# Sliding windows by DMA: the odd rows of the direct batches in 63 small transfers, each released by SyncE's list

## The chip, the core and the metric

The kernel runs on one core of a Trainium2 chip. No compute engine works on the data: everything is moved by DMA. Three engines issue transfers, each through a queue of its own: SyncE (SP in the profile, queue q1), ScalarE (ACT, queue q10) and GpSimd (POOL, queue q0, whose descriptors are written by software and which the change calls the software ring). All three queues feed the same 16 DMA engines. The metric is device microseconds for one execution of the kernel; three runs of the kernel before took 748.2, 749.22 and 749.88 us, with a median of 749.22.

## The reference

```python
batch, length, dim = (32, 4096, 256)      # float32
window_size, stride = 64, 32
n_windows = (length - window_size) // stride + 1        # 127
for i in range(n_windows):
    start = i * stride
    result[:, i] = x[:, start:start + window_size].copy()
```

A batch of the input is 128 blocks of 32 rows; a block is 32 x 256 floats, 32 KB. Window i is blocks i and i+1, so the output is 32 x 127 windows of 64 KB, 266 MB, and nearly every block is written twice: as the second half ("half 1") of one window and as the first half ("half 0") of the next.

## The kernel before

The 32 batches are done in two ways.

**Staged batches.** Twelve batches (`staged`, line 151) are loaded into SBUF, 4 MiB each, one block to a partition (`load`, line 40), and stored from there twice, once as half 0 and once as half 1 of the windows (`store`, line 49). All of this is issued by ScalarE (`ring_s`) in `Staging.run` (line 121): six tiles are loaded, all six are stored, six more are loaded when their tiles are free, and these are stored. Loads and stores are cut into packets of 16 KB. A store has all 128 partitions, although there are only 127 windows, so that its last row falls on one row of a neighbouring batch. The last two staged batches are stored together by `store_pair` (line 102): four stores that count on the semaphore `spilt`, one more store on `ended`, a wait for `spilt`, and then three more stores on `ended`. A store of the pair is 2 MB.

**Direct batches.** The other twenty batches are copied from HBM to HBM. Of the 127 windows of a batch, 112 go in transfers of 16 windows and one half (`halves`, line 174): 16 pieces of 32 KB, 512 KB in all, 14 transfers for each batch, 280 in all. SyncE (`ring_d`) issues them. Of these, 22 hold a row that a staged store overwrites; they are the list `spoilt` (line 175), and SyncE issues them at its end, each after a wait (`wait_stored`, line 114) for the stores beside it. The last two wait for `spilt`.

**Odd rows.** What is left of a direct batch are 15 windows, numbers 48 to 62, as whole rows of 64 KB. GpSimd (`ring_r`) issues them (`remainder`, line 170): one transfer of 15 rows for each batch, with packets of 32 KB or, for four batches, 16 KB; the last batch's 15 rows are split into one transfer of 11 rows and four of 2 rows and one half. That makes 24 transfers, all issued at the start without any wait.

**Order.** SyncE issues one transfer (line 191), then waits for the semaphore `back` (line 192), which the 15-row transfer of the 17th direct batch sets when it has landed, and then issues the other 257 `halves` and the 22 `spoilt`. An issuing engine is held up when its ring is full, so that SyncE and ScalarE issue at the pace of their transfers; the trace shows a median of 84.0 us from the issue of a SyncE transfer to its landing. At the end SyncE waits for all counts (line 199).

## Time and profile before

| what | value |
|---|---|
| runs, median | 749.22 us (748.2 to 749.88) |
| the profiled execution | 747.93 us, its span 746.1 us |
| moved by the DMA engines | 317.50 MB, 426 GB/s over the span |
| q1, SyncE: packets, MB, share of 16 engines' span | 8960, 146.82, 46.0% |
| q10, ScalarE | 10064, 151.00, 47.6% |
| q0, GpSimd | 1280, 19.66, 6.2% |
| SyncE's wait for `back` | 83.2 us |
| from issue to landing, median | SyncE 84.0 us; GpSimd's 15 rows 44.1 us; ScalarE's loads of 4096 KB 121.2 us |

The page counts MB by the packets: a copy from HBM to HBM counts once, and a staged block counts once when it is loaded and once for each store. Small packets of 4 B are the semaphore updates, which travel in the same queues. Besides the views that the page prints, the trace keeps a record of every packet with its queue, start, size and duration; where a number is said to be from the packet records, it is the mean or the sum over these.

### The profile page before, as it was taken

What the parts mean: (1) busy time and instruction counts of PE and PEld (TensorE: products, weight loads), DVE (VectorE), ACT (ScalarE), POOL (GpSimd) and SP (SyncE); (2) the same over time, 40 slices, a digit from 0 to 9 for tenths busy, and PEclk for the clock granted to TensorE, in tenths of its full rate; (3) what the DMA queues carried; (4) which work ended last, traced back from release to release, by engine and by line L of the source; (5) the groups of instructions that cost most, each with busy time, mean ns of one, the idle gap of its engine ahead of it and who ended that gap; (6) DMA issues with size and microseconds to landing.
All of it is one profiled execution on the core that took longest, in us unless ns stands there. A gap on an engine that the chain in (4) does not pass through costs nothing. (4 is left out here: it accounts for less than half of the span.)

```text
span 746.1 us, 413 instructions
## 1 busy us (share of the span) xinstructions
POOL 13.8 (2%) x28
## 2 busy tenths in 40 slices
POOL 7000000000000000000000000000000000000000
DMA  8999999999999999999999999999999999999997
GB/s 365 425 427 417 430 417 432 430 429 435 436 421 432 428 434 434 428 430 432 434 407 427 431 434 429 436 433 428 429 433 432 430 431 431 430 432 433 431 431 336
DMA packets 20306, 317.50 MB, mean 426 GB/s; under 512 B 5880, under 2 KB 5880, under 8 KB 5880
## 3 DMA queue, kind: packets, MB, share of 16 engines
q10 hardware_dynamic: 10064, 151.00, 47.6%
q1 hardware_dynamic: 8960, 146.82, 46.0%
q0 software_dynamic: 1280, 19.66, 6.2%
q14 instruction: 2, 0.02, 0.0%
HBM read 216.79 MB, written 267.12 MB: 649 GB/s over the span
## 5 line engine op out<-in xcount | busy, mean ns | idle before, releaser
L34 POOL DMA_DIRECT2D out_dram<-in_x_dram x24 | 13.6, 571 | 1.1 <-PEq L231 1.1
L217 POOL MEMSET const-float32-0.0<- 128x1 f32 x1 | 0.1, 98 | 0.2 <-issue 0.2
L217 POOL MEMSET const-bfloat16-1.0<- 128x1 bf16 x1 | 0.1, 101 | 0.0
L217 POOL MEMSET const-float32-1.0<- 128x1 f32 x1 | 0.1, 98 | 0.0
L217 POOL MEMSET const-uint8-127<- 128x1 uint8 x1 | 0.1, 98 | 0.0
## 6 DMA issues: line engine op xcount, KB each, us to landing
out_dram<-in_x_dram SPq DMA_DIRECT2D x280, 512.0 KB, 84.0
out_dram<-xb ACTq DMA_DIRECT2D x28, 2048.0 KB, 106.2
xb<-in_x_dram ACTq DMA_DIRECT2D x11, 4096.0 KB, 121.2
out_dram<-xb ACTq DMA_DIRECT2D x10, 4096.0 KB, 120.8
out_dram<-in_x_dram POOLq DMA_DIRECT2D x19, 960.0 KB, 44.1
xb<-in_x_dram ACTq DMA_DIRECT2D x4, 1024.0 KB, 13.9
out_dram<-in_x_dram POOLq DMA_DIRECT2D x1, 704.0 KB, 84.7
out_dram<-in_x_dram POOLq DMA_DIRECT2D x4, 64.0 KB, 69.2
```

The lines of the kernel that those rows point to most:

```text
L34: return q.dma_start(out=self.oap((b * self.nw + w0) * 2 + h, [[2 * blk, n], row]), in_=self.xap(b * self.nb + w0 + h, [[blk, n], row]), m ...
L217: nc = _bacc.Bacc("TRN2", target_bir_lowering=False, num_devices=1)
```

## The change

The 24 transfers of GpSimd become 63 (`drip`): 59 of whole rows, nearly all of them 5 rows, and four of one half of 3 or 5 rows (the entries named a and b in `plan`, whose second half comes later in the list). A row of 64 KB is one packet. The first is issued at once; every other one waits for a semaphore of its own (`marks`), which one of SyncE's `halves` sets when it has landed. The marks are spread evenly over the 258 `halves`, one to each 4.1 of them, so that the last one stands at number 253. SyncE no longer waits for `back`. Every fourth of its `halves` (64 of 258) is cut into packets of 16 KB in place of 32 KB. The staged part and the `spoilt` list are as before.

```diff
-    back = tc.alloc_semaphore("back")
-    total = {done: 0, rest: 0, back: 0}
+    total = {done: 0, rest: 0}
 
     def count(dma, sem):
         dma.then_inc(sem, 16)
-        total[sem] += 16
-
-    def blocks(part):
+        if sem in total:
+            total[sem] += 16
+
+    def blocks(part, piece=DIRECT, sem=done):
         for b, w, half in part:
-            count(c.windows(ring_d, b, w, 16, half), done)
-
-    def remainder(i, b, w, n, half=None, piece=DIRECT):
-        count(c.windows(ring_r, b, w, n, half, piece), back if i == len(direct) - 4 and n == 15 else rest)
-
-    first, last = 48, B - 1
+            count(c.windows(ring_d, b, w, 16, half, piece), sem)
+
+    first = 48
...
+    plan = [(5, "")] * 26 + [(2, ""), (3, "a")] + [(5, "")] * 5 + [(5, "b")] + [(5, "")] * 6
+    plan += [(3, "a")] + [(5, "")] * 2 + [(5, "b")] + [(5, "")] * 19
+    drip, named, at = [], {}, 0
+    for n, name in plan:
+        if name in named:
+            drip.append((*named[name], n, 1))
+            continue
+        b, w = direct[at // 15], first + at % 15
+        drip.append((b, w, n, 0 if name else None))
+        at += n
+        if name:
+            named[name] = b, w
+    assert at == 15 * len(direct)
+    marks = [tc.alloc_semaphore(f"mark{i}") for i in range(len(drip) - 1)]
+    at = [len(halves) * (i + 1) // len(drip) for i in range(len(marks))]
+
     with tc.tile_critical():
         st.run(ring_s)
 
-        pairs = iter([(first + d, half) for d in (0, 2) for half in (0, 1)])
-        for i, b in enumerate(direct[:-1]):
-            if i in (12, 15, 17, 18):
-                w, half = next(pairs)
-                remainder(i, last, w, 2, half, DIRECT // 2)
-            if i == len(direct) - 2:
-                remainder(i, last, first + 4, 11)
-            remainder(i, b, first, 15, piece=DIRECT // 2 if i in (0, 1, 2, 6) else DIRECT)
+        for i, (b, w, n, half) in enumerate(drip):
+            if i:
+                ring_r.wait_ge(marks[i - 1], 16)
+            count(c.windows(ring_r, b, w, n, half, 2 * DIRECT), rest)
         ring_r.drain()
 
-        blocks(halves[:1])
-        ring_d.wait_ge(back, 16)
-        blocks(halves[1:])
+        for i, h in enumerate(halves):
+            sem = marks[at.index(i)] if i in at else done
+            blocks([h], DIRECT if i % 4 != 2 else DIRECT // 2, sem)
```

## The prediction

> **What bounds the kernel now.** I read the page's slices and queues first, since no compute engine works. The row "DMA" is the busy share of the 16 DMA engines in 40 slices.

> ```profile
> span 746.1 us, 413 instructions
> DMA  8999999999999999999999999999999999999997
> GB/s 365 425 427 417 430 417 432 430 429 435 436 421 432 428 434 434 428 430 432 434 407 427 431 434 429 436 433 428 429 433 432 430 431 431 430 432 433 431 431 336
> q10 hardware_dynamic: 10064, 151.00, 47.6%
> q1 hardware_dynamic: 8960, 146.82, 46.0%
> q0 software_dynamic: 1280, 19.66, 6.2%
> ```

> The engines are full from the second slice to the last but one, and the queues' shares add up to 99.8%. The bound is the engines' own rate. The stretches between the kernel's stages show where it falls short (columns: length, POOL busy, PE clock, DMA share, GB/s):

> ```profile
> 0.00:5.00 5.00, 3.69 (x11) 1.00 0.55 210
> 5.00:98.00 93.00, 10.06 (x18) 1.00 1.01 426
> 98.00:132.00 34.00, 0.00 (x0) 1.00 1.00 418
> 132.00:371.00 239.00, 0.00 (x0) 1.00 1.01 431
> 371.00:383.00 12.00, 0.00 (x0) 1.00 1.03 403
> 383.00:738.00 355.00, 0.00 (x0) 1.00 1.01 431
> 738.00:746.10 8.10, 0.00 (x0) 1.00 0.54 216
> ```

> Undisturbed, it runs at 431 GB/s. At that rate 317.50 MB take 736.7 us. The rest, against 431: start 5 x (431-210)/431 = 2.6 us; 5 to 98 us, ScalarE's loads beside GpSimd's rows, 93 x 5/431 = 1.1; 98 to 132, loads beside SyncE's list, 34 x 13/431 = 1.0; 371 to 383, where ScalarE turns from stores to loads, 12 x 28/431 = 0.8; end 8.1 x 215/431 = 4.0. Together 746.2, the span. No edit of order can win more than these 9.5 us, and about 4 of the start and end are latency ahead of the first packet (2.4 us into the span) and behind the last (1.8 us before its end).

> Then who waits:

> ```profile
> SPq L34 <- DMA out_dram<-in_x_dram: 83.2, 1, 83.2
> SPq L34 <- DMA out_dram<-xb: 43.4, 2, 39.9
> SPq L200 <- DMA out_dram<-xb: 40.5, 1, 40.5
> ```

> SyncE stands 83.2 us at `back`. That costs nothing: in that time the other two queues held the engines at a share of 1.01.

> Last, how the engines share themselves. This is 383 to 738 us, with two queues working:

> ```profile
> DMA packets 9736, 152.98 MB, mean 431 GB/s; under 512 B 2835, under 2 KB 2835, under 8 KB 2835
> q1 hardware_dynamic: 4869, 79.83, 52.4%
> q10 hardware_dynamic: 4866, 73.14, 48.1%
> ```

> The two queues sent the same number of packets (4869 and 4866) though not the same bytes: they take turns, packet by packet, and a 4 B semaphore packet is a turn too. This decides in which order the lists end.

> **The change, part by part.** Durations are from the packet records: clean means of 1.213 us for 32 KB, 0.611 for 16 KB, 0.009 for 4 B; two 16 KB packets cost 0.009 us more than one of 32 KB. One packet starts 3 to 4 ns before the last is over, so a packet costs 6 ns beyond its bytes.

> - The wait for `back` goes. The engines were full during it, so 0. If cover failed it would be up to 83.2 us; what is late next is nothing, since SyncE's ring then holds transfers from the start. Bounds: a gain of 0 to 1.1 us (the shortfall of 5 to 98 us, if the way GpSimd's rows run there makes it).
> - Packets. GpSimd's data packets fall from 728 (1280 less 552 of 4 B) to 308 (292 of 64 KB, 16 of 32 KB): -420. SyncE's rise by 64 x 16 = 1024. GpSimd's 4 B packets are 552/24 = 23 a transfer, so 39 more transfers bring 897. Net +1501, 94 an engine; at 6 to 9 ns that is 0.6 to 0.8 us, all on the path, as the engines are full. I take +0.6.
> - A packet of 64 KB is in no trace. By the slope from 16 to 32 KB it takes 0.611 + 3 x 0.602 = 2.42 us, no gain or loss; from below nothing is to be had beyond the 6 ns counted above. From above, the slowest row of 32 KB packets is the first 16 of the run, 1.498 us, 23% over the clean mean: on 18.25 such packets an engine that would be 18.25 x 2.42 x 0.23 = +10 us. Those were an engine's first packets; the clean row is nearer, so 0.
> - GpSimd's waits. Behind each wait stand only GpSimd's own later transfers and its drain; SyncE's last wait needs them. An issue takes 571 ns (24 of them, 13.6 us) and a mark comes every 4.1 transfers, about 11 us, so the list keeps pace. The last mark, number 253 of 258, comes with 5 `halves` and 22 `spoilt` still to go, 27 x 2.4 us = 65 us before the end. Cost 0; without that cover, the 3.7 us that the fastest transfer took to land.
> - The turns. GpSimd now takes a third place in the round now and then, which slows the other two alike. ScalarE has 576 data packets and 53 of 4 B an engine: 629 turns. SyncE has (194 x 2) + (64 x 3) + (22 x 2) = 624. Before, SyncE and GpSimd together had 560 + 80 = 640 against 629, and SyncE ended last by a little. Now ScalarE should, by some 5 to 8 turns (it also starts later), which is its last store, 8 packets of 0.61 us = 4.9 us alone. The engines are full with one queue as well, so the cost is 0. The cover to name: after `spilt` ScalarE has one 2 MB store in its ring, 9 turns, 5.5 us even alone, while a new issue needs about 3 us (first packet 2.4 us into the span, first ScalarE packet 3.9). If that cover goes, some 1 to 3 us appear as a dent about 40 us before the end.
> - The engines' loads. 300 rows on 16 engines are 18.75 rows each: 37.5 halves, before as after. If consecutive engines are dealt out in a ring, both plans give 38 halves to twelve or thirteen engines and 34 to 37 to the others. So the end's skew stays; bounds -1.2 and +2.4 us, one 32 KB packet less or one 64 KB packet more on the engine that ends last. I take 0.
> - The loads' shortfall (1.1 + 1.0 us up to 132 us, 0.8 at the turn). The slow packets there are mostly ScalarE's loads, just after a new load begins, when all 16 engines start on it at nearly the same time. Groups of five engines with a 64 KB packet pull the engines apart earlier than 15 of 16 did. Bounds: all 2.1 gone, or as much again. I take half a gain, -1.0.

> Sum on the profiled execution: 747.93 + 0.6 - 1.0 = 747.5. It lies 1.29 us under the median of the runs; the median becomes 749.22 - 0.4 = 748.8.

> [...]

> **The rivals.**

> - Shortfall gone (faster). The 2.1 us up to 132 us and the 0.8 at the turn were stalls of engines in step, and the drip takes them out: 749.22 + 0.6 - 2.9 = 746.9; one packet less of skew at the end, 745.7. For it: from 383 us on, loads ran beside SyncE's list at 431. Against: from 98 to 132 they did so at 418.
> - The end slips (slower). The engine that ends last gets one 64 KB packet too many, or gets it late: +2.4, and 749.22 + 0.6 + 2.4 = 752.2. It decides if the last slice (336 GB/s) falls below 320. For it: the last 8.1 us already run at half rate. Against: the last mark is 65 us ahead.
> - GpSimd's rows disturb wherever they run (slower). They read each block twice at nearly the same time. If their mere presence costs the 5 GB/s seen from 5 to 98 us, it is now paid over some 690 us: 690 x 5/431 = 8.0, less the 1.1 paid before, +6.9: 749.22 + 0.6 + 6.9 = 756.7. It decides if the middle slices fall under 430. Against: in proportion to the rows moved, the sum stays 1.1.
> - Same five engines (slower). If 5 rows always land on the same five, each of these carries 120 halves in place of 37.5: +82 x 1.21 = 99 us. Against: 15 rows on a fixed 15 would have left one engine 46 us short of work before, and the share at 383 to 738 us is 1.01 of all 16. The 64 KB packet at the cold price, 760, I put with this.
> - It does nothing: the removed wait was covered. That is my forecast's core.

> **How the numbers follow.** A measurement of this kernel can tell about 0.2%, 1.5 us, from no change (747.7 to 750.7). Chances: forecast 0.42, its own range 747.4 to 750.3; shortfall gone 0.25; the end slips 0.18; rows disturb everywhere 0.10; five engines or slow packets 0.05. Faster: 0.25 and 0.06 of the forecast's lower edge, 0.31. Same: 0.36. Slower: 0.33. A range of 745.7 to 753.0 leaves out the last two cases and a little of the others, 0.19.

> **What would show it.** Right: q0's work spread over all slices, 431 in the middle; q1 and q10 with the same packet counts in any stretch; SP's 83.2 us wait gone without a change of the time; ScalarE's store landing last. Wrong: middle slices under 430, last slices thin, or a span below 744.

## The result and the profile after

The changed kernel took 850.33 us (849.87 to 851.52) against 749.22 for the kernel before: 1.135 times as long, 95% interval 1.1335 to 1.1366, or 101.1 us more. Its profiled execution took 849.87 us, its span 848.1 us. The forecast was 748.8 with a range up to 753.0. The time lies at the rival "same five engines", which had been given 0.05 together with slow packets and would give 749.22 + 0.6 + 99 = 849.

The page after, its slices and queues:

```profile
span 848.1 us, 451 instructions
DMA  9999999999999999999999799999998898843382
GB/s 371 423 430 434 429 424 429 430 435 432 426 428 436 424 424 436 428 424 423 422 402 382 305 349 402 393 378 370 351 417 349 355 392 335 331 195 150 134 358 123
q1 hardware_dynamic: 9984, 146.82, 43.0%
q10 hardware_dynamic: 10064, 151.00, 41.9%
q0 software_dynamic: 2016, 19.67, 5.5%
```

The bytes are the same. For the first half the engines run as before, at some 430 GB/s; from there on they fall off. The stretches say it more sharply (length, POOL busy, PE clock, DMA share, GB/s):

```profile
5.00:98.00 93.00, 3.65 (x7) 1.00 1.01 428
98.00:132.00 34.00, 1.57 (x3) 1.00 1.00 425
132.00:371.00 239.00, 9.92 (x19) 1.00 1.01 429
...
437.00:740.00 303.00, 12.53 (x24) 1.00 0.92 367
740.00:778.00 38.00, 1.57 (x3) 1.00 0.48 186
778.00:798.00 20.00, 0.52 (x1) 1.00 0.31 134
798.00:830.00 32.00, 0.00 (x0) 1.00 0.71 293
830.00:848.10 18.10, 0.00 (x0) 1.00 0.24 102
```

The line to stop at is 778 to 798 us: a share of 0.31 of 16 engines is five engines, working at their full rate (134 GB/s is 5/16 of 430), while eleven stand idle. Against 431 GB/s the five last stretches lose 45, 22, 14, 10 and 14 us, about 105 in all, where the end of the kernel before lost 4.

These are SyncE's waits after, the ones that answer to those shown of before. The 83.2 us at `back` are gone, and that bought nothing:

```profile
SPq L34 <- DMA out_dram<-xb: 66.7, 4, 44.4
SPq L209 <- DMA out_dram<-xb: 36.5, 1, 36.5
```

How many engines lag can be read from the semaphores. Each mark is set by one transfer of SyncE, 16 pieces of 32 KB with 16 updates (4480 packets of 4 B for 280 transfers), and the trace keeps the time of each update. Which engine one came from it does not say; they are read here as one from each engine. These are the 16 updates of some marks of the changed kernel, in order, as us after the first of them:

```
mark at   the 16 updates, us after the first
 15.1     0.0 0.0 0.0 0.1 0.2 0.2 0.2 0.3 0.3 0.5 0.8   2.1  2.2  2.3  2.4  2.4
 24.7     0.0 0.1 0.1 0.1 0.2 0.2 0.2 0.2 0.3 0.4 0.6   4.7  4.8  4.8  4.8  5.3
 34.9     0.0 0.1 0.1 0.2 0.3 0.3 0.4 0.4 0.5 0.6 0.8   6.8  6.9  7.0  7.2  7.7
 44.8     0.0 0.0 0.1 0.2 0.2 0.2 0.3 0.3 0.3 0.4 0.6   9.3  9.3  9.4  9.6 10.0
423.9     0.0 0.1 0.2 0.2 0.3 1.0 1.0 1.3 1.7 2.2 2.7  88.1 91.1 91.3 93.2 93.6
690.7     0.0 0.1 0.2 0.2 0.2 0.2 0.3 0.3 0.3 0.3 0.6  82.2 88.3 89.3 89.7 90.0
```

Eleven engines are together and five fall behind, by one 64 KB packet (2.4 us) more with every transfer of GpSimd. So every transfer gives its five rows to the same five engines. The lag grows to some 90 us and stops there. What stops it can be counted from the packet records: SyncE's packets that are issued and not yet done when an issue ends. In the kernel before this number rises while an issue takes 0.59 us (median from 85 to 110 us); from 130 to 600 us it stands at 1110 to 1121 (median 1112), while an issue takes 2.39 us and a transfer 84 us to land: that is what lies in a ring. In the changed kernel it reaches 1090 at 31 us and is down to 354 to 437 from 437 to 690 us (median 398), not far above five sixteenths of 1112, 348; from 437 to 740 us SyncE issues a transfer only every 3.0 us (101 in 303 us). On this count the five have a full ring, SyncE's issue is held up for all 16, and the eleven run dry. The marked transfers show it: one whose issue ended at 111.4 us had its first update 55.5 us later and its last 95.2 us later; one whose issue ended at 420.1 us had them after 3.7 and 97.2 us. From then on eleven engines have next to no queue, and five have a full one. That is why the first half of the profile looks healthy.

### The profile page after: what moved, and what is told of

It is laid out like the page before. It is cut to its first block, busy times and chain, and to the rows that moved or that the text cites. A ratio compares the mean times of both kernels' runs of the same rounds, so it can differ in the third digit from the quotient of the medians.

```text
span 848.1 us, 451 instructions
## 1 busy us (share of the span) xinstructions
POOL 33.2 (4%) x67
## 3 DMA queue, kind: packets, MB, share of 16 engines
q1 hardware_dynamic: 9984, 146.82, 43.0%
q10 hardware_dynamic: 10064, 151.00, 41.9%
## 4 chain that ended last, share of the span: by engine, by line
another core or an unknown queue 79%; DMA 5%; POOL 4%; issue 3%; SPq 1%; POOLq 0%
DMA out_dram<-in_x_dram 5%; POOL out_dram L34 4%; SPq L34 1%; POOLq L198 0%; SPq L240 0%; SPq L191 0%
## 5 line engine op out<-in xcount | busy, mean ns | idle before, releaser
L34 POOL DMA_DIRECT2D out_dram<-in_x_dram x63 | 33.0, 524 | 748.0 <-DMA out_dram<-in_x_dram 747.0
```

The costliest lines, as they stand in the source:

```text
L34: return q.dma_start(out=self.oap((b * self.nw + w0) * 2 + h, [[2 * blk, n], row]), in_=self.xap(b * self.nb + w0 + h, [[blk, n], row]), m ...
```

## Experiments

What was open is why the deal of rows to engines, which turned in the kernel before, stood still here: the packet, the wait before each transfer, or the number of rows. On the chips of the experiments the kernel before took 746.3 to 746.7 us, not 749.22, so every run is read against the kernel before beside it. The changed kernel itself was not run there. A time without an interval is one execution.

### Packets of 32 KB

```diff
-            count(c.windows(ring_r, b, w, n, half, 2 * DIRECT), rest)
+            count(c.windows(ring_r, b, w, n, half, DIRECT), rest)
```

> The changed kernel with GpSimd's rows cut into packets of 32 KB again; the 63 transfers, their waits and SyncE's list stay. All theories agree that 60 x 64 KB rows fall on the same five engines in the changed kernel (120 halves in place of 37.5, 82 x 1.21 = 99 us). They differ in why the deal stopped turning. Packet theory (a row that is one 64 KB packet is always dealt from the same engine): 749 us here, within 3. Wait theory (a transfer that is issued alone, after a wait, starts the deal anew): 850, unchanged. Row theory (a transfer of 5 rows always takes the same five): 850, unchanged.

751.92 us beside 746.73. The 98 us are gone with the packet, and with them the wait theory and the row theory: waits and five rows are still there. The first three marks show the deal move on by five engines with each transfer: five engines are some 2.4 us behind the others at the first mark, ten at the second, fifteen at the third. But 5.2 us stay. The stretches of this run show five engines once more, only for a short while at the end:

```profile
700.00:740.00 40.00, 0.00 (x0) 1.00 1.00 426
742.00:745.00 3.00, 0.00 (x0) 1.00 0.32 137
```

The marks date it. Up to 317 us the 16 updates lie within 4.5 us; then five engines fall behind, to about 10 us at 512 us, where the eleven others lie within 3. The transfers released at that time are those of one half, entries a and b of `plan`. Their rows are 32 KB, so with packets of 32 KB they still have one packet to a row. If they fall on the same first engines, the fullest carries 4 of these 16 halves in place of 1, which is 3 x 1.21 = 3.6 of the 5.2 us.

### No waits

```diff
-    marks = [tc.alloc_semaphore(f"mark{i}") for i in range(len(drip) - 1)]
-    at = [len(halves) * (i + 1) // len(drip) for i in range(len(marks))]
...
         for i, (b, w, n, half) in enumerate(drip):
-            if i:
-                ring_r.wait_ge(marks[i - 1], 16)
             count(c.windows(ring_r, b, w, n, half, 2 * DIRECT), rest)
...
         for i, h in enumerate(halves):
-            sem = marks[at.index(i)] if i in at else done
-            blocks([h], DIRECT if i % 4 != 2 else DIRECT // 2, sem)
+            blocks([h], DIRECT if i % 4 != 2 else DIRECT // 2, done)
```

> The changed kernel with GpSimd's 63 transfers all issued at the start, no wait and no mark; 64 KB packets and SyncE's cut list stay. Wait theory: the deal turns again, 749 us, within 3. Packet theory and row theory: the same five engines still carry 120 halves, 850 us, within 10.

850.42 us beside 746.73, 103.7 us more; with the waits it was 101.1 more, on another chip. The deal stood still here too, though no transfer waited for another to land. The lag comes earlier, and so does the hole, but the sum of the work on the five is the same:

```profile
98.00:371.00 273.00, 0.00 (x0) 1.00 0.84 347
...
800.00:810.00 10.00, 0.00 (x0) 1.00 0.32 136
```

### 15 rows in packets of 64 KB

```diff
-                remainder(i, last, first + 4, 11)
-            remainder(i, b, first, 15, piece=DIRECT // 2 if i in (0, 1, 2, 6) else DIRECT)
+                remainder(i, last, first + 4, 11, piece=2 * DIRECT)
+            remainder(i, b, first, 15, piece=2 * DIRECT)
```

> The kernel before with its transfers of 15 and 11 rows in packets of 64 KB. Packet theory: the same 15 engines each time, one engine is left without rows and the others carry 40 halves in place of 38: 749.2 + 2 x 1.21 = 751.6 us. Wait theory and row theory: the deal turns as before, 748 to 750.

757.1 us beside 746.73. The direction is that of the packet theory, but the size is 10.4 us where 2.4 were expected. One engine is left without rows: towards the end the share is 15 of 16, 0.94.

```profile
5.00:98.00 93.00, 9.16 (x18) 1.00 1.00 405
...
690.00:720.00 30.00, 0.00 (x0) 1.00 0.94 403
720.00:738.00 18.00, 0.00 (x0) 1.00 0.95 396
738.00:755.00 17.00, 0.00 (x0) 1.00 0.62 266
```

The first line holds part of what the expectation lacked: with 64 KB packets on 15 engines beside ScalarE's loads the first stretch ran at 405 GB/s (426 in the kernel before), 93 x 21/431 = 4.5 us. The last line holds another part, 17 x 165/431 = 6.5 us, where the end of the kernel before lost 4: ScalarE's last packet ended 13 us behind SyncE's, at 753.5 us. The parts are read from single executions and do not add up to the last microsecond.

### 15 rows with waits

```diff
...
+    marks = [tc.alloc_semaphore(f"mark{i}") for i in range(23)]
+    sent = []
...
     def remainder(i, b, w, n, half=None, piece=DIRECT):
-        count(c.windows(ring_r, b, w, n, half, piece), back if i == len(direct) - 4 and n == 15 else rest)
+        if sent:
+            ring_r.wait_ge(marks[len(sent) - 1], 16)
+        sent.append(n)
+        count(c.windows(ring_r, b, w, n, half, piece), rest)
...
-        blocks(halves[:1])
-        ring_d.wait_ge(back, 16)
-        blocks(halves[1:])
+        at = [len(halves) * (i + 1) // 24 for i in range(23)]
+        for i, h in enumerate(halves):
+            blocks([h], marks[at.index(i)] if i in at else done)
```

> The kernel before with its 24 transfers (15 rows, 32 and 16 KB packets) each released by a mark of SyncE's list, 23 waits evenly spread, and SyncE's wait for back gone; SyncE's packets stay at 32 KB. Wait theory: the same 15 engines each time, one left without rows, 751.6 us. Packet theory and row theory: the deal turns, 748 to 750.

754.68 us beside 746.73: no theory had that. The deal did turn: the updates of the 23 marks stay within 7.3 us of each other, and no engine is far in front of the rest. The loss is another one. In this run SyncE's packets are uncut, its list is early, and it stood 119.1 us at the staged stores. That led to the next runs.

### Every odd row in two packets

```diff
-            count(c.windows(ring_r, b, w, n, half, 2 * DIRECT), rest)
+            count(c.windows(ring_r, b, w, n, half, DIRECT if half is None else DIRECT // 2), rest)
```

> The changed kernel with every odd row in two packets: whole rows as 2 x 32 KB, the four transfers of one half as 2 x 16 KB. Form theory (a transfer of GpSimd with one packet to a row is always dealt to the same first engines; with two packets to a row the deal turns): no engine group lags any more, the marks' 16 landings stay within 4 us of each other, and what is left of the change is worth what the forecast's other terms say, +0.6 for packets and up to -2.1 of the loads' shortfall: between 2 us faster and 1 us slower than the kernel before on this chip. If the drip costs something in itself, as in the first run with 32 KB packets (+5.2), it stays 3 to 5 us slower.

746.25 us beside 746.43: ratio 0.9999, interval 0.999 to 1.0007. With this one expression the 101 us are gone, and the rest of the change, taken together, is worth nothing. From the run with packets of 32 KB this one differs in the four transfers of one half alone, and the 5.2 us are gone too. The 16 updates of each of the 62 marks lie within 5.1 us. The stretches and, from 383 to 680 us, the queues:

```profile
5.00:98.00 93.00, 4.63 (x8) 1.00 1.01 430
98.00:132.00 34.00, 1.74 (x3) 1.00 1.00 424
132.00:371.00 239.00, 12.72 (x22) 1.00 1.01 430
371.00:383.00 12.00, 0.58 (x1) 1.00 1.02 423
383.00:600.00 217.00, 11.58 (x20) 1.00 1.01 431
```

```profile
q10 hardware_dynamic: 4014, 60.72, 47.7%
q1 hardware_dynamic: 4017, 58.48, 46.0%
q0 software_dynamic: 1319, 8.62, 6.9%
```

SyncE and ScalarE send the same number of packets also when GpSimd sends packets of its own: the turns hold. SyncE's last packet ended at 740.5 us of the span and ScalarE's at 742.9.

### Two halves of 32 KB

```diff
-            count(c.windows(ring_r, b, w, n, half, 2 * DIRECT), rest)
+            for h in (0, 1) if half is None else (half,):
+                count(c.windows(ring_r, b, w, n, h, DIRECT), rest)
```

> The changed kernel with each whole-row transfer replaced by two transfers of the same rows, half 0 and half 1, each row one packet of 32 KB; the wait stands before the first of the two. Form theory: one packet to a row, so the same five engines as with 64 KB: about 850 us. Size theory (it is the length of 64 KB that stops the turning): 749, within 4.

848.54 us beside 746.43. The packets are 32 KB, as in runs that turned; the rows have one packet each, and the same five engines lag. So it is the form of the transfer, one packet to a row, and not the length of the packet. What makes the form matter, no run shows.

```profile
437.00:740.00 303.00, 23.83 (x46) 1.00 0.91 367
778.00:798.00 20.00, 1.04 (x2) 1.00 0.32 138
```

### Sixteen transfers with one packet to a row

The kernel with every odd row in two packets, with `2 * DIRECT` for the first 16 transfers.

> The changed kernel with every odd row in two packets, except that the first 16 transfers (80 rows) keep one packet of 64 KB to a row. Form theory with the price by load: five engines carry 32 + 220 x 2 / 16 = 59.5 halves, 22 more than 37.5: 22 x 1.21 = 26.6 us on top of the run with every row in two packets, 773 us, within 3. If the lag of the five engines is made good as long as it fits in the rings (under 80 us): 747.

774.92 us beside 746.33: 28.6 us more, where 26.6 were worked out. The lag grew to about 42 us by the 18th mark and then stayed. It fitted in the rings (84 us from issue to landing in the kernel before), and from 300 to 700 us the engines were full (430 GB/s), yet it is paid in full at the end: eleven engines ended at about 752 us, five between 768.6 and 770.9.

```profile
300.00:700.00 400.00, 21.07 (x37) 1.00 1.01 430
700.00:740.00 40.00, 0.57 (x1) 1.00 0.65 253
...
755.00:768.00 13.00, 0.00 (x0) 1.00 0.32 136
```

### The list uncut, the rows up front, and 15 rows with the cut list

Three runs price the other parts, each as an edit of a kernel above. First, the run with every odd row in two packets, and SyncE's list uncut:

```diff
-            blocks([h], DIRECT if i % 4 != 2 else DIRECT // 2, sem)
+            blocks([h], DIRECT, sem)
```

> As the run with every odd row in two packets, but SyncE's list not cut, all its packets 32 KB. Turn theory: SyncE then has 560 turns an engine against ScalarE's 629 and is through its list early, so that ScalarE ends alone: about 2 us slower than with the cut list, SyncE waiting on the staged stores for over 100 us. If the cut does nothing, the two are the same, or this one is 0.4 us faster for 1024 packets less.

751.61 us, 1.0069 times the kernel before (1.0054 to 1.0084). With fewer and larger packets of SyncE the kernel is slower. SyncE stood 120.0 us at the staged stores (59.6 with the cut list), as the turn theory says, and its last packet ended 13 us before ScalarE's. But most of the 5 us lies elsewhere, in stretches where all engines were busy and slower (93 x 9/431 + 217 x 4/431 = 4.0 us against the cut list):

```profile
5.00:98.00 93.00, 4.63 (x8) 1.00 1.01 421
...
383.00:600.00 217.00, 11.60 (x21) 1.00 1.01 427
```

Second, every odd row in two packets and the list cut, but all 63 transfers issued at the start, without waits and marks:

> As the run with every odd row in two packets, but GpSimd's 63 transfers all issued at the start, with no wait and no mark; the list stays cut. If spreading the rows over the run is what relieves the loads, this one has the shortfall of the first 130 us again and is 1.5 us slower than the spread one; if not, both are the same within 0.5 us.

752.4 us, 1.0077 times (1.0064 to 1.0091). GpSimd's last packet ended at 267.9 us, and up to there the engines ran at 416 to 418 GB/s, after it at 431:

```profile
5.00:98.00 93.00, 32.96 (x58) 1.00 1.01 416
98.00:260.00 162.00, 0.00 (x0) 1.00 1.01 418
260.00:371.00 111.00, 0.00 (x0) 1.00 1.01 431
```

Third, the run with 15 rows and waits, with the cut list (`DIRECT if i % 4 != 2 else DIRECT // 2`):

> The kernel before with its 24 transfers (15 rows, two or four packets to a row) each released by a mark, as in the run with 15 rows and waits, and now every fourth of SyncE's halves cut into 16 KB packets. If it is the cut that keeps the engines out of stalls and the two long lists level, this one is within 1 us of the kernel before or up to 1 us faster (116 packets of 4 B an engine fewer than with 63 transfers, 0.6 us); if small transfers of five rows are needed for it, it stays 3 us or more slower.

749.42 us beside 746.33, 1.004 times (1.0026 to 1.0054). Between the two expectations: the cut won most of the loss of the uncut one (754.68 beside 746.73), and 3 us stayed, with 428 GB/s from 383 to 600 us where the run with five rows had 431. No version came out faster than the kernel before.

## Why the prediction was wrong

The step that failed is "The engines' loads": "If consecutive engines are dealt out in a ring, both plans give 38 halves to twelve or thirteen engines". That ring was the author's assumption, and no run shows it for rows of one packet. With two packets to a row the deal moved on (five engines behind at the first mark, ten at the second, fifteen at the third in the run with packets of 32 KB); with one it stood still, and 848.5 to 850.4 us came of it. The term was taken at 0, with bounds of -1.2 and +2.4 us, and it came to some 101. The five engines carried 120 halves each on the mean in place of 37.5, and 82 x 1.21 = 99 us is what came, within 2 us. So the price of the rival was right and its chance was not.

Its chance was set low by evidence that did not bear on it. The share of 1.01 in the kernel before was read as a sign that transfers of 15 rows with two packets to a row are dealt in a ring. Their deal does turn (the 23 marks of the run with 15 rows and waits stay within 7.3 us), but the share is a blunt sign: the run with 15 rows in packets of 64 KB, with one engine left without rows, had 1.01 from 98 to 600 us as well, and only its last 65 us (0.94) gave it away. The change altered just that form, and the step took the deal over to it. The packet of 64 KB was looked at for its duration alone.

What the traces show for rows of one packet: 5 rows on five fixed engines (0.31 from 778 to 798 us, and five updates 2.4 us later with every transfer), 15 rows with one engine left out (0.94). They do not say which engines these are.

The other steps:

- The wait for `back`, 0: right where the rows turn and are spread over the run (ratio 0.9999 without it). It was not tried alone. With the wait gone, the list cut and the rows in 63 transfers up front, the kernel was 6 us slower, and which of these costs that is open.
- Packets, +0.6: nearly right. GpSimd's 4 B packets are not 23 a transfer, and not all of them are semaphore updates: the changed kernel has 1708 of them and 63 x 16 = 1008 updates. The counts fit 16 a transfer, and one more for each data packet that an engine without rows lacks: 16 + 11 = 27 for five rows of one packet, 16 + 22 = 38 for five rows of two. Over all transfers that gives the 552 of the kernel before, the 1708 of the changed kernel and the 2408 of the run that turned. An engine has (1708 - 552 - 420 + 1024)/16 = 110 packets more in the changed kernel, 0.7 us at 6 ns each (9 ns, of which 3 overlap), and (2408 - 552 - 112 + 1024)/16 = 173 in the run that turned, 1.0 us.
- A 64 KB packet, 2.42 us by the slope: right, 2.436 on the mean of 292.
- GpSimd's waits, 0: right. They come to 747.0 us in the trace, and the kernel without them is no faster.
- The turns: right. From 132 to 371 us SyncE sent 3274 packets and ScalarE 3273, and ScalarE ended last by 2.4 us in the run that turned (4.9 expected). With one queue the engines were nearly full: 0.95 from 738 to 746 us of the run with the list uncut, where ScalarE's queue was the last one working. What was not foreseen is how much the cut list is worth beside it, 0.7%.
- The loads' shortfall, half a gain: the run that turned lost 0.2 + 0.6 us up to 132 us, where the kernel before lost 2.1, and paid about 1.0 for packets. On balance it was no faster.

Of the other rivals, "rows disturb wherever they run" did not happen where the rows turned and were spread: the middle stretches ran at 430 and 431 GB/s. Something like it is seen in the 416 to 418 GB/s of the run with the rows up front. Its cause was not tried.

## What to carry to other kernels

Before small transfers are counted on to spread over the DMA engines, look at the form of each, rows and packets to a row: evidence from another form did not carry over here (746.25 us with two packets to a row, 848.5 to 850.4 with one). The uneven deal hid behind full engines while the rings held the lag (430 GB/s from 300 to 700 us with a lag of 42 us), so look at the DMA share at the end (0.31 is five of sixteen) and at the spread of one transfer's 16 semaphore updates. Its price here was the load of the fullest engines, whether the lag fitted in the rings (28.6 us where 26.6 were worked out) or not (101.1 where 99 were).
